# A bidirectional HGRN2 and Conformer encoder layer: the first step of a half head's preparation queued on VectorE behind the level-64 key update of the half head in work

## The chip, the cores and the metric

One core of one Trainium2 chip runs the whole layer as one program. The metric is the device time of one execution in microseconds (us). The kernel before was run three times: 1732.26, 1730.40 and 1727.42 us, a median of 1730.4 us.

## The reference, cut to what matters

The layer mixes 1024 positions of width 1024 in two parallel branches and then applies a gated feed-forward block. The part that this change concerns is the branch called HGRN2, a gated linear recurrence that is run over the sequence in both directions for each of 8 heads of width 128:

```python
def _chunk_gated_scan(q, k, v, lf):
    # S_t = diag(f_t) S_{t-1} + k_t v_t^T,  o_t = S_t^T q_t
    ...
    def step(state, inp):
        qb, kb, vb, lfb = inp
        a = jnp.cumsum(lfb, axis=2)
        diff = a[:, :, :, None, :] - a[:, :, None, :, :]
        decay = jnp.where(tril, jnp.exp(jnp.minimum(diff, 0.0)), 0.0)
        scores = jnp.einsum("bhtk,bhsk,bhtsk->bhts", qb, kb, decay)
        o = (jnp.einsum("bhts,bhsv->bhtv", scores, vb)
             + jnp.einsum("bhtk,bhkv->bhtv", qb * jnp.exp(a), state))
        ...
def _bi_hgrn2(q, v, z_fwd, z_bwd, lb_fwd, lb_bwd):
    ...
    o_fwd = _chunk_gated_scan(qh, heads(k_f), vh, heads(lf_f))
    o_bwd = flip(_chunk_gated_scan(flip(qh), flip(heads(k_b)), flip(vh), flip(heads(lf_b))))
    return o_fwd + o_bwd
```

The decay between two positions is the product of all forget gates between them. All else in the layer (projections, convolutions, feed-forward block, norms) is untouched by the change.

## The kernel before, in words

The kernel runs in stages: projections of the input with the convolution branch, then the scan of the 8 heads with the remaining dense projections between its pieces, then the merge, the output projection and the feed-forward block.

**The scan.** A head's 1024 positions are two halves of 512; the loop goes over 16 half heads, numbered 0 to 15 here. The chip's buffers carry the numbers of the program: the keys of half heads 3, 4, 5 and 6 are kG_787, kG_836, kG_896 and kG_949, their queries qF_823, qF_888, qF_936 and qF_1006. Each half head goes through a doubling scheme. At level h (1, 2, 4, ..., 64) pairs of neighbouring blocks of h positions meet: the keys are multiplied by the decay to the block's edge (`double_keys`, VectorE, line L1143 because all go through the helper `tt`), the queries likewise (`double_queries`), and the block totals `tb` are multiplied in pairs (`totals`). The updates of one half head's keys are a chain, each on the one before. In a row of the profile `kG<-kG,tb` is a key update, `qF<-qF,tb` a query update, `tb<-tb` or `tb<-f` totals.

**Who waits for it.** TensorE (PE) multiplies keys and queries of a level. For levels up to 16 it reads copies that ScalarE makes (`woven`, tiles A, L1175) before VectorE's next update; the products of the first four go into one PSUM bank `sc` (`level`, L1194), those of levels 8 and 16 into `ob`. Levels 32 and 64 are read from kG and qF themselves (`blocks`, L1280). After the level-64 key update, TensorE transposes the finished keys of both directions (`scan_states`, L1320, `tr<-ident,kG`), ScalarE copies the transposes, and TensorE forms the chunks' states from them (L1329).

**Three half heads at a time.** While half head i is in work (`scan_levels`, `scan_states`), half head i + 1 is in preparation (`scan_base`, held by the class `Base` as `ahead`) and half head i + 2 has its inputs loaded and makes its first step (`following`). The first step of `scan_base` ends at its first `yield`: it scales the two directions' keys (L1223), adds them (A<-kG), makes the level-1 queries and keys and the first totals (tb<-f). `between(n)` is called after each piece of half head i: it issues one or two pieces of dense projections (`dense.fill(FILL)`), one piece of the previous head's output, and one step of `ahead` for n below 4, of `following` at n = 4.

**What sets the order.** TensorE's order is the order in which the code is written (`manual_schedule`). For the other engines a scheduler orders the instructions of the program by its own costs, within what data and buffers allow; each engine then runs its instructions strictly in that order, and waits at the one in front. So the rows in which VectorE runs the steps of the three half heads are the scheduler's choice, unless an instruction is tied to another.

Of the kernel before, what the change touches and what calls it, by code (L numbers as in the profile page):

```python
# [37 lines left out]
def view(t, off, dims):  # L38

    return bass.AP(  # L40
        tensor=t.tensor,
        offset=t.offset + off,
        ap=[list(t.ap[0])] + [list(d) for d in dims],
    )
# [3 lines left out]
def tile_hybrid_encoder(  # L48
# [24 lines left out]
    V, A, G, T = nc.vector, nc.scalar, nc.gpsimd, nc.tensor  # L73
# [20 lines left out]
    def nm(s):  # L94
        uid[0] += 1
        return f"{s}_{uid[0]}"
# [3 lines left out]
    def bank(tag):  # L100
        return ps.tile([P, H], F32, tag=tag, name=nm(tag), bufs=BANKS[tag])

    def page(pool, tag, bufs, dt=F32):
        return pool.tile([P, H], dt, tag=tag, name=nm(tag), bufs=bufs)
# [64 lines left out]
    class Weights:  # L169
# [3 lines left out]
        def __init__(self, steps):  # L173
            self.parts = {}
            self.steps, self.wait = steps(self.parts), 0
            self.tick()
# [963 lines left out]
    G.memset(none, 0.0)  # L1140

    def tt(o, a, b, op=ALU.mult):
        V.tensor_tensor(o, a, b, op=op)  # L1143

    kscale = cp.tile([P, 2 * NH], F32, name="kscale")
    V.tensor_scalar(kscale, lbw[:, 3, :], DK**-0.5, None, op0=ALU.mult)
# [1 line left out]
    def c4(t):  # L1148
        return t.rearrange("p (c t) -> p c t", c=4)
# [18 lines left out]
    def pairs(t, h, other=H):  # L1168

        return view(t, 0, [[other + h, 2], [2 * h, H // (2 * h)], [1, h]])  # L1170

    def woven(t, h):

        t_h = page(hp, "A", 8)
        A.copy(pairs(t_h, h, 0), pairs(t, h))  # L1175
        return t_h

    def slot(b, n):
        return b[:, n * P : (n + 1) * P]

    def near(t):
        return t.rearrange("p (c t) -> p c t", c=4)

    def over(m):
        return view(m, 0, [[0, 4], [1, 32]])

    def each():
        for c in range(4):
            for g in range(0, P, 32):
                yield c * P + g, slice(g, g + 32), slice(32 * c, 32 * c + 32)  # L1190

    def level(b, A_t, Q_t):
        for at, g, o in each():
            T.matmul(b[g, o], A_t[:, at : at + 32], Q_t(at), start=True, stop=True)  # L1194

    def row(t):
        return lambda at: t[:, at : at + 32]

    def double_keys(kG, tb, h):
        n, nb = H // (2 * h), H // h  # L1200
        tt(pairs(kG, h), pairs(kG, h), view(tb, 1, [[nb - 1, 2], [2, n], [0, h]]))

    def double_queries(qF, q, tb, h):
        n, nb = H // (2 * h), H // h
        tt(pairs(qF, h), q, view(tb, nb + 1, [[-(nb + 1), 2], [2, n], [0, h]]))

    def totals(tb, h, to=None):
        n, nb = H // (2 * h), H // h
        tn = None
        if to is None:  # L1210
            tn = hp.tile([P, 2, n], F32, tag=f"tb{h}", name=nm("tb"), bufs=1 if h < 8 else 2)
            to = view(tn, 0, [[n, 2], [1, n]])
        tt(to, view(tb, 0, [[nb, 2], [2, n]]), view(tb, 1, [[nb, 2], [2, n]]))
        return tn

    def scan_base(ins):


        q, f, kG, ks = ins
        qF = hp.tile([P, 2, H], F32, tag="qF", name=nm("qF"), bufs=4)  # L1220
        D_t = hp.tile([P, 4, 32], F32, tag="D", name=nm("D"), bufs=3)
        for d in range(2):
            V.tensor_scalar(kG[:, d, :], kG[:, d, :], ks[:, d : d + 1], None, op0=ALU.mult)  # L1223
        k_d, Q1 = page(hp, "A", 8), page(hp, "A", 8)
        tt(k_d, kG[:, 0, :], kG[:, 1, :], ALU.add)
        A1 = woven(kG, 1)
        odd = H // 2
        tt(
            pairs(Q1, 1, 0),
            view(q, 0, [[1, 2], [2, odd], [1, 1]]),  # L1230
            view(f, H, [[1 - H, 2], [2, odd], [1, 1]]),
        )
        tt(
            view(qF, 1, [[H - 1, 2], [2, odd]]),
            view(q, 1, [[-1, 2], [2, odd]]),
            view(f, H + 1, [[-(H + 1), 2], [2, odd]]),
        )
        double_keys(kG, f, 1)
        double_queries(qF, pairs(Q1, 1, 0), f, 1)
        tb = totals(f, 1)  # L1240
        yield
        A2, Q2 = woven(kG, 2), woven(qF, 2)
        double_keys(kG, tb, 2)
        double_queries(qF, pairs(qF, 2), tb, 2)
        tb = totals(tb, 2)
        A4, Q4 = woven(kG, 4), woven(qF, 4)
        yield
        b = bank("sc")
        for n, (k_t, q_t) in enumerate(((k_d, q), (A1, Q1), (A2, Q2), (A4, Q4))):
            level(slot(b, n), k_t, row(q_t))  # L1250
        double_keys(kG, tb, 4)
        double_queries(qF, pairs(qF, 4), tb, 4)
        tb = totals(tb, 4)
        A8, Q8 = woven(kG, 8), woven(qF, 8)
        yield
        A.copy(D_t, near(slot(b, 3)))
        for n, m in enumerate((m_d, m_1, m_2)):
            V.copy_predicated(D_t, over(m), near(slot(b, n)))
        double_keys(kG, tb, 8)
        double_queries(qF, pairs(qF, 8), tb, 8)  # L1260
        tb = totals(tb, 8)
        A16, Q16 = woven(kG, 16), woven(qF, 16)
        yield
        double_keys(kG, tb, 16)
        double_queries(qF, pairs(qF, 16), tb, 16)
        tb = totals(tb, 16)
        yield qF, kG, tb, D_t, A8, Q8, A16, Q16

    def scan_levels(base, S_t, Tt):


        qF, kG, tb, D_t, A8, Q8, A16, Q16 = base

        def blocks(b, h):

            for c in range(0, H, P):
                for s0 in range(0, P, h):
                    t0 = s0 ^ h
                    d = s0 // h % 2
                    T.matmul(  # L1280
                        b[s0 : s0 + h, c + t0 : c + t0 + h],
                        kG[:, d, c + s0 : c + s0 + h],
                        qF[:, 1 - d, c + t0 : c + t0 + h],
                        start=True,
                        stop=True,
                    )

        def double(tb, h, to=None):
            double_keys(kG, tb, h)
            double_queries(qF, pairs(qF, h), tb, h)  # L1290
            return totals(tb, h, to)

        b = bank("ob")
        level(slot(b, 0), A8, row(Q8))
        level(slot(b, 1), A16, row(Q16))
        S_b = bank("sc")
        for at, g, _ in each():
            T.matmul(S_b[g, at : at + 32], none, none, start=True, stop=True)
        blocks(S_b, 32)
        for n, m in enumerate((m_8, m_16)):  # L1300
            V.copy_predicated(D_t, over(m), near(slot(b, n)))
        tb = double(tb, 32)
        yield
        yield
        b = S_b
        blocks(b, 64)
        double(tb, 64, view(Tt, 0, [[4, 2], [1, 4]]))
        A.copy(S_t, c4(b))
        for g in range(0, P, 32):
            G.dma_start(S_t[g : g + 32, :, g : g + 32], D_t[g : g + 32])  # L1310
        yield
# [92 lines left out]

    class Base:
        def __init__(self, ins):
            self.gen, self.val = scan_base(ins), None

        def step(self, n):
            while n > 0 and self.val is None:  # L1410
                self.val = next(self.gen)
                n -= 1

        def result(self):
# [33 lines left out]
    for h in range(NH):  # L1448
        Tt = hp.tile([P, 2, 2, 4], F32, tag="Tt", name=nm("Tt"), bufs=4)
        Sf = [hp.tile([P, 4, DK], F32, tag="st", name=nm("Sf"), bufs=4) for _ in range(2)]  # L1450
        Sb = [hp.tile([P, 4, DK], F32, tag="st", name=nm("Sb"), bufs=4) for _ in range(2)]
        kept = []
        for half in range(2):
# [13 lines left out]
            for n, _ in enumerate(scan_levels(base, S_t, Tt[:, half])):  # L1467
                if n == 1:
                    b = bank("tr")
# [5 lines left out]
            qF, kG = base[:2]  # L1475
# [514 lines left out]
    n = starts[-1] - per_seven - 12  # L1990
# [50 lines left out]
```

## Time and profile before

| quantity | value |
|---|---|
| the profiled execution's own time | 1733.97 us |
| its span, first to last instruction | 1732.2 us |
| ScalarE busy in the span | 826.1 us (48%) |
| GpSimd busy in the span | 206.5 us (12%) |
| mean granted TensorE clock | 0.996 |
| bytes read from and written to HBM | 201.40 and 87.03 MB |

The profiled execution is a run of its own beside the three timed ones; 1.8 us of its time lie outside the span. TensorE's rows need care: matmuls overlap in the pipeline and their ends are modelled, so an interval of idle TensorE is what is left after a modelled end. On VectorE one instruction starts some 0.08 us before the profile's end of the one before it, so what an instruction costs its queue is the distance of two starts, not the duration shown. The window from 495 to 865 us holds the scan.

### The profile page before, as it was taken

How to read it: one execution, taken by the hardware profiler on the slowest of the kernel's cores; microseconds unless marked ns; L12 is line 12 of the kernel's file. 1: busy time of each engine (PE TensorE's matmuls, PEld its weight loads, DVE VectorE, ACT ScalarE, POOL GpSimd, SP SyncE). 2: the span in 40 equal slices, each digit the busy share in tenths (PEclk: the TensorE clock that was granted, in tenths of full speed). 3: DMA queues.
4: the chain of work that ended last, by engine and by line, in shares of the span. 5: the costliest groups of instructions: out<-in, count | busy, mean ns of one | idle time of the engine just before them, and what ended most of it. 6: DMA issues, size and time to landing. Idle time of an engine off the chain costs nothing. (4 is left out here: it accounts for less than half of the span.)

```text
span 1732.2 us, 30782 instructions
## 1 busy us (share of the span) xinstructions
PE 1704.5 (98%) x11902; PEld 1416.5 (82%) x11902; DVE 1255.2 (72%) x1937; ACT 826.1 (48%) x1544; POOL 206.5 (12%) x249
## 2 busy tenths in 40 slices
PE   8999999999999999999999999999999999999998
PEld 6878888788788888888878888888888788888787
DVE  4599999746778888888566466666767776657864
ACT  7444443334566777776442245444334443542334
POOL 2211111100001111111100002011111111000110
PEclk9999999999999999999999999999999999999999
DMA  8778888854673434436579466567777777783842
GB/s 287 236 173 183 192 194 192 199 165 151 207 238 101 134 126 132 127 114 211 185 258 318 143 206 196 146 149 160 158 168 168 161 179 162 226 263 105 215 93 98
DMA packets 336585, 308.29 MB, mean 178 GB/s; under 512 B 17070, under 2 KB 248630, under 8 KB 336438
## 3 DMA queue, kind: packets, MB, share of 16 engines
q1 hardware_dynamic: 289590, 267.51, 48.9%
q0 software_dynamic: 46848, 38.81, 15.3%
q8 instruction: 93, 1.52, 0.4%
q14 instruction: 54, 0.44, 0.1%
HBM read 201.40 MB, written 87.03 MB: 167 GB/s over the span
## 5 line engine op out<-in xcount | busy, mean ns | idle before, releaser
L148 PE MATMUL mm<-hx,wp 128*128 128x512 f32 x1068 | 429.0, 402 | 5.9 <-ACT tm L850 2.5
L150 PE MATMUL mm<-hx,wp 128*128 128x512 f32 x1068 | 418.4, 392 | 1.0 <-DVE wp L124 0.9
L149 PE MATMUL mm<-hx,wp 128*128 128x512 f32 x1068 | 417.8, 391 | 0.5 <-DVE hx L124 0.5
L124 ACT CAST wp<-wr 128x1024 fp32r<-128x1024 f32 (+2 forms) x147 | 147.4, 1004 | 270.6 <-DMA wr<-wr 115.3
L148 PEld LDWEIGHTS mm<-hx,wp 128*128 128x128 f32 x1068 | 201.3, 188 | 50.8 <-ACT su L439 3.2
L150 PEld LDWEIGHTS mm<-hx,wp 128*128 128x128 f32 x1068 | 201.2, 188 | 47.2 <-DVE wp L124 4.4
L149 PEld LDWEIGHTS mm<-hx,wp 128*128 128x128 f32 x1068 | 201.6, 189 | 40.7 <-DVE hx L124 1.4
L124 DVE TENSOR_TENSOR wp<-wr,wp 128x1024 fp32r<-128x1024 f32 (+2 forms) x145 | 169.5, 1170 | 82.0 <-ACT wp L124 79.1
L1038 DVE SCALAR_TENSOR_TENSOR acc<-gl,v_b,acc 128x1024 f32<-128x1024 f32 x120 | 149.0, 1278 | 0.4
L439 ACT COPY su<-mm 128x512 f32<-128x512 f32 x82 | 47.7, 581 | 58.8 <-PE mm L150 58.7
L148 PE MATMUL tr<-hx,wp 128*128 128x512 f32 x180 | 70.5, 392 | 0.0
L150 PE MATMUL tr<-hx,wp 128*128 128x512 f32 x180 | 70.0, 389 | 0.0
L149 PE MATMUL tr<-hx,wp 128*128 128x512 f32 x180 | 70.0, 389 | 0.0
L1310 POOL DMA_DIRECT2D S<-D x64 | 35.5, 560 | 286.7 <-ACT jk L1375 127.7
L1143 DVE TENSOR_TENSOR qF<-qF,tb 128x512 f32<-128x512 f32 x96 | 65.5, 686 | 4.6 <-ACT A L1175 4.6
L1637 DVE SCALAR_TENSOR_TENSOR tm<-gp,v_a,tm 128x512 f32<-128x512 f32 x88 | 66.0, 750 | 3.8 <-ACT tm L1635 2.0
L124 ACT CAST wq<-sw 128x1024 fp32r<-128x1024 f32 x41 | 43.2, 1054 | 52.3 <-PE mm L149 43.0
L1143 DVE TENSOR_TENSOR kG<-kG,tb 128x512 f32<-128x512 f32 x96 | 65.2, 686 | 0.3
L148 PE MATMUL mm<-hy,wp 128*128 128x512 f32 x164 | 64.2, 391 | 0.0
L148 PE MATMUL sc<-hy,wq 128*128 128x512 f32 x164 | 64.2, 391 | 0.0
L150 PE MATMUL sc<-hy,wq 128*128 128x512 f32 x164 | 63.8, 389 | 0.0
L149 PE MATMUL mm<-hy,wp 128*128 128x512 f32 x164 | 63.8, 389 | 0.0
(373 smaller groups left out, 3679.4 us busy)
## 6 DMA issues: line engine op xcount, KB each, us to landing
wr<-in_w_in_dram SPq DMA_DIRECT2D x48, 512.0 KB, 4.3
wr<-in_ffn_w_up_dram SPq DMA_DIRECT2D x22, 512.0 KB, 6.2
sw<-in_w_in_dram SPq DMA_DIRECT2D x38, 256.0 KB
d_g<-ft SPq DMA_DIRECT2D x38, 256.0 KB, 3.4
sw<-in_ffn_w_up_dram SPq DMA_DIRECT2D x38, 256.0 KB, 4.1
sw<-in_ffn_w_up_dram POOLq DMA_DIRECT2D x19, 512.0 KB, 7.9
wr<-sw POOLq DMA_DIRECT2D x32, 256.0 KB, 3.8
wr<-wr POOLq DMA_DIRECT2D x32, 256.0 KB, 4.3
```

Source lines behind the costliest of these rows:

```text
L124: parts = A.copy(hi, src), eng.tensor_tensor(lo, src, hi.bitcast(F32), op=ALU.subtract)
L148: T.matmul(acc, whi[:, k, :], ahi, start=first, stop=False, skip_group_check=again)
L149: T.matmul(acc, whi[:, k, :], alo, start=False, stop=False, skip_group_check=again)
L150: T.matmul(acc, wlo[:, k, :], ahi, start=False, stop=last, skip_group_check=again)
L439: A.copy(t, acc)
L1038: V.scalar_tensor_tensor(acc, g[:, k : k + S], tap(k), acc, op0=ALU.mult, op1=ALU.add)
L1143: V.tensor_tensor(o, a, b, op=op)
L1310: G.dma_start(S_t[g : g + 32, :, g : g + 32], D_t[g : g + 32])
L1637: V.scalar_tensor_tensor(c, g[:, o + k : o + k + H], vec("fdw", k * NF + j), c, op0=ALU.mult, op1=ALU.add,)
```

## The change

The level-64 key update of the half head in work is remembered in a list of one entry. When a `Base` makes its first step, all instructions of that step that go to VectorE are tied behind it in VectorE's order. The tie is one of order alone: no semaphore is waited for, and no instruction is added or taken away.

```diff
     def tt(o, a, b, op=ALU.mult):
-        V.tensor_tensor(o, a, b, op=op)
+        return V.tensor_tensor(o, a, b, op=op)
+
+    last_keys = []
...
     def double_keys(kG, tb, h):
         n, nb = H // (2 * h), H // h
-        tt(pairs(kG, h), pairs(kG, h), view(tb, 1, [[nb - 1, 2], [2, n], [0, h]]))
+        return tt(pairs(kG, h), pairs(kG, h), view(tb, 1, [[nb - 1, 2], [2, n], [0, h]]))
...
-        def double(tb, h, to=None):
-            double_keys(kG, tb, h)
+        def double(tb, h, to=None, kept=None):
+            done = double_keys(kG, tb, h)
+            if kept is not None:
+                kept[:] = [done]
             double_queries(qF, pairs(qF, h), tb, h)
             return totals(tb, h, to)
...
-        double(tb, 64, view(Tt, 0, [[4, 2], [1, 4]]))
+        double(tb, 64, view(Tt, 0, [[4, 2], [1, 4]]), last_keys)
...
     class Base:
         def __init__(self, ins):
-            self.gen, self.val = scan_base(ins), None
+            self.gen, self.val, self.first = scan_base(ins), None, True

         def step(self, n):
             while n > 0 and self.val is None:
-                self.val = next(self.gen)
+                if self.first and last_keys:
+                    with tc.issue_after(last_keys[0].ins):
+                        self.val = next(self.gen)
+                else:
+                    self.val = next(self.gen)
+                self.first = False
                 n -= 1
```

The scheduler then orders VectorE and ScalarE anew throughout the scan; TensorE's and GpSimd's orders stay, and on the DMA queue of SP a few neighbouring loads and stores change places. Three places of VectorE's order show it.

**First place: the rows that end at half head 3's level-64 key update** (kG_787<-kG_787,tb_903), near 589 us of the trace. Half head 4 (kG_836, qF_888) is in preparation; f_895, q_894, tb_941, tb_964, qF_936, kG_896 and A_938 belong to half head 5's first step. Before:

```order
L1143 TENSOR_TENSOR kG_836_5324<-kG_836_5324,tb_911_5832 128x2x64x4
L124 TENSOR_TENSOR wp_907_5812<-wr_905_5809,wp_906_5811 128x1024
L1143 TENSOR_TENSOR qF_888_5695<-qF_888_5695,tb_911_5832 128x2x64x4
L1143 TENSOR_TENSOR kG_836_5324<-kG_836_5324,tb_919_5932 128x2x32x8
L1143 TENSOR_TENSOR qF_936_6041<-q_894_5710,f_895_5711 128x2x256
L1143 TENSOR_TENSOR tb_941_6054<-f_895_5711 128x512
L1143 TENSOR_TENSOR tb_964_6185<-tb_941_6054 128x256
L1398 SCALAR_TENSOR_TENSOR ev_917_5862<-tr_916_5857,v_a_1084,og_864_5495 128x512
L1143 TENSOR_TENSOR qF_888_5695<-qF_888_5695,tb_919_5932 128x2x32x8
L1143 TENSOR_TENSOR kG_836_5324<-kG_836_5324,tb_924_5974 128x2x16x16
L1143 TENSOR_TENSOR A_938_6045<-kG_896_5712 128x512
L1143 TENSOR_TENSOR kG_787_4993<-kG_787_4993,tb_903_5798 128x2x4x64
```

With the change:

```order
L1143 TENSOR_TENSOR kG_836_5324<-kG_836_5324,tb_893_5708 128x2x128x2
L1143 TENSOR_TENSOR qF_888_5695<-qF_888_5695,tb_893_5708 128x2x128x2
L124 TENSOR_TENSOR wp_907_5812<-wr_905_5809,wp_906_5811 128x1024
L1143 TENSOR_TENSOR kG_836_5324<-kG_836_5324,tb_911_5832 128x2x64x4
L1143 TENSOR_TENSOR qF_888_5695<-qF_888_5695,tb_911_5832 128x2x64x4
L1143 TENSOR_TENSOR kG_836_5324<-kG_836_5324,tb_919_5932 128x2x32x8
L1402 SCALAR_TENSOR_TENSOR ev_917_5862<-tr_916_5857,v_a_1084,og_864_5495 128x512
L1143 TENSOR_TENSOR qF_888_5695<-qF_888_5695,tb_919_5932 128x2x32x8
L1143 TENSOR_TENSOR kG_836_5324<-kG_836_5324,tb_924_5974 128x2x16x16
L1143 TENSOR_TENSOR qF_888_5695<-qF_888_5695,tb_924_5974 128x2x16x16
L1143 TENSOR_TENSOR kG_787_4993<-kG_787_4993,tb_903_5798 128x2x4x64
```

Four instructions of half head 5 (qF_936, tb_941, tb_964, A_938) are gone from ahead of the update. Two of half head 4 have come in: its level-2 key update (kG_836<-kG_836,tb_893), which before stood further up, ahead of half head 3's level-32 update, and its level-16 query update (qF_888<-qF_888,tb_924), which before stood behind.

**Second place: half head 5's first step itself**, on VectorE. Before, its first scaling stood directly behind half head 4's last totals (Tt_942):

```order
L1143 TENSOR_TENSOR kG_836_5324<-kG_836_5324,tb_893_5708 128x2x128x2
L1143 TENSOR_TENSOR tb_933_6012<-tb_924_5974 128x32
L1143 TENSOR_TENSOR tb_956_6149<-tb_933_6012 128x16
L1143 TENSOR_TENSOR Tt_942_6056<-tb_956_6149 128x8
L1223 TENSOR_SCALAR kG_896_5712<-kG_896_5712,kscale_4332 128x512
L1335 COPY Sf_830_5318<-sc_886_5664 128x128
```

With the change it stands behind the level-64 key update of half head 3:

```order
L1143 TENSOR_TENSOR kG_787_4993<-kG_787_4993,tb_903_5798 128x2x4x64
L1143 TENSOR_TENSOR qF_823_5302<-qF_823_5302,tb_903_5798 128x2x4x64
L1260 COPY_PREDICATED D_889_5696<-m_d_1507,sc_918_5865 128x128
L1402 SCALAR_TENSOR_TENSOR ev_923_5965<-tr_922_5960,v_a_1084,og_875_5620 128x512
L1260 COPY_PREDICATED D_889_5696<-m_1_1508,sc_918_5865 128x128
L1225 TENSOR_SCALAR kG_896_5712<-kG_896_5712,kscale_4332 128x512
L1260 COPY_PREDICATED D_889_5696<-m_2_1509,sc_918_5865 128x128
L1225 TENSOR_SCALAR kG_896_5712<-kG_896_5712,kscale_4332 128x512
L1143 TENSOR_TENSOR qF_936_6041<-q_894_5710,f_895_5711 128x2x256
```

The whole step has moved some twenty rows down, past half head 3's last updates.

**Third place: half head 6's level 2** (kG_949 and qF_1006 with tb_1011), while half head 5 (kG_896, qF_936) is in work, near 627 us. The query update there is followed by ScalarE's copy of it, which TensorE's products at L1194 read. Before:

```order
L1143 TENSOR_TENSOR kG_896_5712<-kG_896_5712,tb_998_6401 128x2x8x32
L1301 COPY_PREDICATED D_937_6042<-m_16_1511,ob_1019_6477 128x128
L1143 TENSOR_TENSOR qF_936_6041<-qF_936_6041,tb_998_6401 128x2x8x32
L1143 TENSOR_TENSOR qF_1006_6444<-qF_1006_6444,tb_1011_6457 128x2x128x2
L1143 TENSOR_TENSOR kG_949_6063<-kG_949_6063,tb_1024_6571 128x2x64x4
```

With the change:

```order
L1143 TENSOR_TENSOR kG_896_5712<-kG_896_5712,tb_998_6401 128x2x8x32
L1305 COPY_PREDICATED D_937_6042<-m_16_1511,ob_1019_6477 128x128
L1143 TENSOR_TENSOR qF_936_6041<-qF_936_6041,tb_998_6401 128x2x8x32
L1143 TENSOR_TENSOR kG_949_6063<-kG_949_6063,tb_1011_6457 128x2x128x2
L1143 TENSOR_TENSOR qF_1006_6444<-qF_1006_6444,tb_1011_6457 128x2x128x2
L1143 TENSOR_TENSOR kG_949_6063<-kG_949_6063,tb_1024_6571 128x2x64x4
```

The level-2 key update of half head 6, which before was done in the half head's first burst, now stands directly ahead of the query update. Over the whole program, the level-2 key update of the half head in preparation falls from ahead of the level-32 update of the half head in work to behind it in 3 of 14 cases (half heads 4, 6 and 8).

## The prediction

> **What bounds the kernel now.** I read the page first, then the busy times by stretch, then TensorE's waits, then VectorE's timeline at the waits found.
>
> ```profile
> span 1732.2 us, 30782 instructions
> PE 1704.5 (98%) x11902; PEld 1416.5 (82%) x11902; DVE 1255.2 (72%) x1937; ACT 826.1 (48%) x1544; POOL 206.5 (12%) x249
> ```
>
> TensorE (PE) is busy in all but 28 us of the span. A change of VectorE's order can take away idle TensorE time or add some, and nothing else. So the next view is where the idle time lies in the scan (us from the start, length, then the busy time of PE, PEld, DVE, ACT, POOL, the granted clock, DMA share, GB/s):
>
> ```profile
> 495.00:865.00 370.00, 366.16 (x5882) 314.74 (x5882) 303.45 (x660) 258.45 (x586) 48.50 (x78) 1.00 0.45 143
> 580.00:600.00 20.00, 17.97 (x339) 15.13 (x337) 19.83 (x44) 15.30 (x30) 2.25 (x4) 1.00 0.50 163
> 620.00:640.00 20.00, 19.56 (x345) 16.41 (x344) 16.30 (x33) 17.42 (x36) 2.26 (x5) 1.00 0.45 146
> 720.00:740.00 20.00, 18.62 (x254) 15.95 (x254) 18.38 (x44) 12.58 (x23) 2.26 (x4) 1.00 0.49 151
> PE tr L1320 <- DVE kG L1143: 3.8, 3, 2.0
> 589.83 0.66 PE L1320 MATMUL tr<-ident,kG 128*128 128x128 f32 x4 [2.03 <-DVE kG L1143]
> 634.08 0.66 PE L1320 MATMUL tr<-ident,kG 128*128 128x128 f32 x4 [0.44 <-DVE kG L1143]
> 721.56 0.66 PE L1320 MATMUL tr<-ident,kG 128*128 128x128 f32 x4 [1.38 <-DVE kG L1143]
> ```
>
> In the 370 us of the scan TensorE idles 370.00 - 366.16 = 3.84 us. The waits name it all: three times the transposes of finished keys (L1320) wait for VectorE's key update, 2.03 + 0.44 + 1.38 = 3.85 us. In the other 13 half heads this wait does not show. VectorE is busy 303.45 of 370 us: it has room on average, and is late only at these three places. What the change can win in the scan is therefore at most some 3.9 us, or 0.22% of the time. A difference of under 0.3% (5.2 us of 1730.4) is about what a measurement of this kernel can't tell from no change; the three runs before alone lie 4.8 us apart.
>
> **The change part by part.** No instruction is added or removed; the eight VectorE instructions of a first step (and with them later totals) move behind the level-64 key update. What such an instruction costs the queue is the distance of two starts:
>
> ```profile
> 569.88 0.69 DVE L1143 TENSOR_TENSOR kG<-kG,tb 128x512 f32<-128x512 f32 x1
> 570.49 0.40 DVE L1143 TENSOR_TENSOR tb<-tb 128x32 f32<-128x32 f32 x2
> ...
> 584.96 0.69 DVE L1143 TENSOR_TENSOR qF<-q,f 128x512 f32<-128x512 f32 x1
> 585.56 0.69 DVE L1143 TENSOR_TENSOR tb<-f 128x512 f32<-128x512 f32 x1
> 586.28 0.42 DVE L1143 TENSOR_TENSOR tb<-tb 128x256 f32<-128x256 f32 x1
> 586.62 0.74 DVE L1398 SCALAR_TENSOR_TENSOR ev<-tr,v_a,og 128x512 f32<-128x512 f32 x1
> ...
> 588.48 0.69 DVE L1143 TENSOR_TENSOR A<-kG 128x512 f32<-128x512 f32 x1
> 589.09 0.68 DVE L1143 TENSOR_TENSOR kG<-kG,tb 128x512 f32<-128x512 f32 x1
> ...
> 590.49 0.69 DVE L1143 TENSOR_TENSOR qF<-qF,tb 128x512 f32<-128x512 f32 x1
> 591.09 0.75 DVE L1398 SCALAR_TENSOR_TENSOR ev<-tr,v_a,og 128x512 f32<-128x512 f32 x1
> ```
>
> *First wait (half head 3).* The update that TensorE waits for starts at 589.09 and ends at 589.77; the transposes start at 589.83. Ahead of it four instructions leave: qF<-q,f 585.56 - 584.96 = 0.60, tb<-f 586.28 - 585.56 = 0.72, tb<-tb 586.62 - 586.28 = 0.34, A<-kG 589.09 - 588.48 = 0.61; together 2.27 us. Two come in, as the first place of the order shows: half head 4's level-2 key update (here at 569.88, 570.49 - 569.88 = 0.61) and its level-16 query update (here at 590.49, 591.09 - 590.49 = 0.60); together 1.21. Net 1.06 us earlier: the wait shrinks from 2.03 to 0.97. It does not go.
>
> *Second wait (half head 5).* The same three instructions of the following half head leave (0.60, 0.60 and 0.33 by the rows below), and one level-2 key update comes in (0.61): net 0.92 earlier, more than the 0.44 waited. Gain 0.44.
>
> ```profile
> 628.74 0.69 DVE L1143 TENSOR_TENSOR qF<-q,f 128x512 f32<-128x512 f32 x1
> 629.34 0.68 DVE L1143 TENSOR_TENSOR qF<-qF,tb 128x512 f32<-128x512 f32 x1
> 629.94 0.69 DVE L1143 TENSOR_TENSOR tb<-f 128x512 f32<-128x512 f32 x1
> 630.54 0.68 DVE L1143 TENSOR_TENSOR kG<-kG,tb 128x512 f32<-128x512 f32 x1
> ...
> 631.81 0.41 DVE L1143 TENSOR_TENSOR tb<-tb 128x256 f32<-128x256 f32 x1
> 632.14 0.68 DVE L1143 TENSOR_TENSOR qF<-qF,tb 128x512 f32<-128x512 f32 x1
> ```
>
> *Third wait (half head 9).* The same three leave and nothing comes in (the level-2 key update stood there already): some 1.5 us earlier against 1.38 waited. Gain 1.38. Sum of the gains: 1.06 + 0.44 + 1.38 = 2.88 us.
>
> *What is late next.* Each first step now starts later, and TensorE needs its fruits one half head on, in the products at L1194. The last of them reads ScalarE's copy of the level-2-updated queries. At two places this copy comes just in time already:
>
> ```profile
> 628.31 0.62 ACT L1175 COPY A<-qF 128x512 f32<-128x512 f32 x1 [1.17 <-PE tr L1396]
> 628.57 1.07 PE L1194 MATMUL sc<-A,A 128*32 128x32 f32 x96
> 760.09 0.60 ACT L1175 COPY A<-qF 128x512 f32<-128x512 f32 x1
> 760.33 1.05 PE L1194 MATMUL sc<-A,A 128*32 128x32 f32 x96
> ```
>
> The 96 products are three groups of some 0.29 us; the third starts near 628.57 + 0.58 = 629.15, and the copy ended at 628.31 + 0.62 = 628.93: 0.22 us of cover. At 760 it is 760.91 against 760.69, again 0.22. At the first of the two (half head 6, third place of the order) a level-2 key update of 0.61 us now stands directly ahead of the query update that is copied: the products wait 0.61 - 0.22 = some 0.4 us. At the second the order keeps that update where it was, but TensorE arrives earlier by what it has won; if VectorE and ScalarE do not move with it, it waits. The bounds of both: nothing, if the copies move up along with TensorE as their own waits for TensorE end sooner; at most the 2.88 us won, all handed back. I take the one count that the rows give, 0.4, for both: 0.8 us is given back.
>
> *ScalarE and DMA.* ScalarE's copies of the moved step follow it; ScalarE is busy 258.45 of 370 us and its other work (bank copies L802, weight casts L124) changes place with them by one or two rows, hidden by three PSUM banks of products in flight; without that cover one row late costs some 0.6 us, a copy's length. On SP's queue a few neighbouring loads and stores swap; the loads are for half heads not yet begun, so I cost them at nothing; a late one would cost at most one issue slot.
>
> Sum: 2.88 - 0.8 = 2.1 us saved. Against the profiled execution (1733.97 us, of it 1732.2 span) that is 1731.9; this execution lies 3.6 us over the median of the runs shown, so against the median it is 1730.4 - 2.1 = **1728.3 us**. The unknown cost leaves 0 to 3.9 us saved, 1726.5 to 1730.4, and two medians of three runs scatter by some 2 us more.
>
> **The rivals.**
>
> *Faster by more than 0.3%.* It needs more than the scan holds. Behind the scan TensorE stalls near 900 us and runs slowly after it:
>
> ```profile
> 899.00:901.00 2.00, 1.23 (x5) 0.51 (x3) 0.43 (x1) 1.08 (x2) 0.00 (x0) 1.00 0.95 315
> 901.00:907.00 6.00, 5.54 (x17) 4.05 (x17) 5.62 (x10) 1.63 (x3) 0.00 (x0) 0.72 1.09 357
> ```
>
> Idle 0.77 + 0.46 us, and at a granted clock of 0.72 a further 6 x 0.28 = 1.7: 2.9 us. Should all three waits go, nothing come back, and these loads and splits, released by a scan that VectorE finishes earlier, be ready in time, 3.85 + 2.9 = 6.8 us are saved: 1723.6. For it: VectorE's queue loses long stops (below). Against it: TensorE also arrives earlier, and the DMA engines are full there (share 0.95 and 1.09). [...]
>
> *Slower: the preparation is late in every half head.* The first step, some 4.6 us of VectorE (two scalings of 0.5 and six instructions of 0.6), starts later: half head 5's second scaling ran at 577.79 (row below) and would now stand behind 589.09. If the level-2 key update then falls in front of the copied query update everywhere, and no cover is left, each of 14 half heads loses 0.61: 8.5 - 2.88 = 5.7 us slower, 1736.1. The point from which it decides is the order: the update falls behind the level-32 update in 3 of 14. Against it speaks too that VectorE idles 370 - 303.45 = 66.5 us in the scan, 4 us per half head.
>
> *Slower by the same place: the queue stops at its head.*
>
> ```profile
> 577.79 0.49 DVE L1223 TENSOR_SCALAR kG<-kG,kscale 128x512 f32<-128x512 f32 x1 [3.51 <-ACT kG L1162]
> DVE kG L1223 <- ACT kG L1162: 25.3, 13, 4.6
> 585.10 0.69 PE L1280 MATMUL sc<-qF,kG 128*64 128x64 f32 x16
> ```
>
> VectorE stood 3.51 us for the scaling of a first step because ScalarE had not made its keys, with other work behind it; 25.3 us in 13 such waits. The level-64 update has a wait of its own: TensorE must have read the old keys (L1280). At half head 3 that ended at 585.79, the update starts at 589.09 and would start 1.06 us earlier: over 2 us of cover. If the cover were gone, the whole first step would stand behind it; I give it no time of its own, the rival above holds it. [...]
>
> *It does nothing for the time.* What is won at the three waits comes back in full at L1194 and at the next key updates: 1730.4.
>
> **How the numbers follow.** The forecast with its own range of 1726 to 1731: 0.55. All handed back: 0.10. Faster beyond 0.3% (under 1725.2): 0.23. Slower beyond 0.3% (over 1735.6): 0.12. So same is 0.65. The range 1722 to 1734 reaches into the faster rival as far as all three waits and the stall near 900 gone, and leaves the far ends of both rivals out, less than 2 in 10.
>
> **What would show it.** In the changed kernel's profile the waits of L1320 for kG should sum to about 1 us, most of it at half head 3 near 588 us; the two others should be gone. New waits of L1194 for copies A should show near 628 and 759 us, some 0.4 us each. TensorE's idle time in the scan should fall from 3.84 to about 2 us, VectorE's waits of L1223 for ScalarE well below 25.3 us, and the stages behind 865 us should be the same length. I am wrong if L1320 still waits 2 us at half head 3, if L1194 waits at most half heads, or if the time changes behind the scan.

## The result, and the profile after

The changed kernel took 1725.72 us (median of 22 runs, 1723.88 to 1734.86), the kernel before, in runs beside it, 1730.0 us (22 runs, 1726.81 to 1734.81). The ratio is 0.9979 with a 95% interval of 0.9971 to 0.9986: by it 3.6 us less, between 2.4 and 5.0 (the two medians lie 4.3 us apart). A second measurement of the same pair gave 0.9988 (0.9978 to 0.9997): 2.1 us less. Both are smaller than 0.3%, and both are clear of zero. A saving of 2.1 us and a time of 1728.3 us had been forecast; the median lies 2.6 us under that time, inside the wide range of 1722 to 1734 us and just below the narrower one of 1726 to 1731.

The page of the changed kernel's profile begins so:

```profile
span 1722.5 us, 30765 instructions
PE 1698.2 (99%) x11902; PEld 1414.3 (82%) x11902; DVE 1255.7 (73%) x1937; ACT 826.1 (48%) x1544; POOL 207.6 (12%) x249
```

The work is the same to the instruction (11902 matmuls, 1937 instructions of VectorE); only idle time has gone. The span is 9.7 us under that of the profile before, more than the medians differ, so the two profiled executions are not to be compared as a whole. The scan is: its window (columns as in the prediction: busy time of PE, PEld, DVE, ACT, POOL, clock, DMA share, GB/s), and TensorE's waits in it (engine, line, releaser: us in total, times, longest):

```profile
495.00:865.00 370.00, 368.08 (x5900) 316.67 (x5899) 301.18 (x657) 258.66 (x589) 49.68 (x78) 1.00 0.45 144
PE tr L1324 <- DVE kG L1143: 1.2, 2, 1.0
PE sc L1196 <- ACT A L1177: 0.8, 2, 0.5
```

TensorE idles 370.00 - 368.08 = 1.92 us where it idled 3.84. L1324 is what was L1320 before (the transposes of finished keys), L1196 what was L1194 (the products of copies A). TensorE's timeline at the places of the prediction:

```profile
586.94 0.66 PE L1324 MATMUL tr<-ident,kG 128*128 128x128 f32 x4 [1.01 <-DVE kG L1143]
...
626.86 0.46 PE L1196 MATMUL sc<-A,A 128*32 128x32 f32 x32 [0.28 <-ACT A L1177]
...
631.17 0.60 PE L1324 MATMUL tr<-ident,kG 128*128 128x128 f32 x4
...
717.25 0.66 PE L1324 MATMUL tr<-ident,kG 128*128 128x128 f32 x4
...
757.26 0.46 PE L1196 MATMUL sc<-A,A 128*32 128x32 f32 x32 [0.48 <-ACT A L1177]
...
761.90 0.66 PE L1324 MATMUL tr<-ident,kG 128*128 128x128 f32 x4 [0.16 <-DVE kG L1143]
```

At half head 3 the wait of 2.03 us is down to 1.01. At half heads 5 (631.17) and 9 (717.25) the rows have no wait any more, where there were 0.44 and 1.38. Two new waits for ScalarE's copies stand at 626.86 and 757.26, and one of 0.16 us at half head 11. VectorE's queue ahead of the first of these places reads, in its timeline:

```profile
580.44 1.22 DVE L124 TENSOR_TENSOR wp<-wr,wp 128x1024 fp32r<-128x1024 f32 x1
581.58 0.68 DVE L1143 TENSOR_TENSOR kG<-kG,tb 128x512 f32<-128x512 f32 x1
...
584.82 0.68 DVE L1143 TENSOR_TENSOR kG<-kG,tb 128x512 f32<-128x512 f32 x1
585.59 0.69 DVE L1143 TENSOR_TENSOR qF<-qF,tb 128x512 f32<-128x512 f32 x1
586.20 0.68 DVE L1143 TENSOR_TENSOR kG<-kG,tb 128x512 f32<-128x512 f32 x1
```

The last row is the level-64 key update of half head 3; the transposes start at its end. None of half head 5's first step stands ahead of it any more, and the level-16 query update of half head 4 does (585.59, 0.61 us to the next start). In this execution the whole scan lies 1.9 us earlier than in the one before (its first transposes, below), so of 589.09 - 586.20 = 2.89 us some 1.0 is the queue's own.

The queue does not run through without a stop. Ahead of these rows VectorE stands at the row f<-f for ScalarE, before and after:

```profile
579.60 0.69 DVE L1165 TENSOR_SCALAR f<-f 128x1024 f32<-128x1024 f32 x1 [0.77 <-ACT f L1164]
```

```profile
577.42 0.69 DVE L1167 TENSOR_SCALAR f<-f 128x1024 f32<-128x1024 f32 x1 [1.73 <-ACT f L1166]
```

From that row to the key update it is 589.09 - 579.60 = 9.49 us before and 586.20 - 577.42 = 8.78 us after, 0.71 us less. The other 0.3 us come from the stop: its end lies 8.20 us ahead of the moment when TensorE is ready for the transposes (589.83 - 2.03 = 587.80) before, and 8.51 us ahead of it (586.94 - 1.01 = 585.93) after.

VectorE's stops changed place rather than amount. Its waits over the whole run, after:

```profile
DVE qF L1143 <- ACT A L1177: 13.0, 10, 2.8
DVE f L1167 <- ACT f L1166: 11.2, 6, 3.6
DVE D L1305 <- PE ob L1196: 8.5, 5, 2.5
DVE kG L1225 <- ACT kG L1164: 4.0, 2, 3.5
```

The stop at the scalings fell from 25.3 to 4.0 us, and the other three rows have grown (the wait of qF for A was 4.6 us before, that of f 6.1, and the one of D had no row): VectorE stands for ScalarE, and at D for TensorE's bank `ob`, at a later instruction instead. Its busy time is 1255.7 us against 1255.2.

A length that does not depend on the window's edges is the distance from the first to the last transposes of keys. The grouped rows of that line (duration min/median/max in ns, then first and last start) before and after:

```profile
L1320 PE MATMUL mm<-ident,kG x64: 272/273/273, 526.9 to 852.1; 128*128 128x128 f32 x64
```

```profile
L1324 PE MATMUL mm<-ident,kG x64: 272/273/273, 525.0 to 848.7; 128*128 128x128 f32 x64
```

852.1 - 526.9 = 325.2 us before, 848.7 - 525.0 = 323.7 after: the scan is 1.5 us shorter by starts, 1.9 by idle time (whose ends are modelled). This distance serves below as the scan's length.

### The profile page after: what moved, and what is told of

Its sections match the earlier page's. It is cut to its first block, busy times and chain, and to the rows that moved or that the text cites. A ratio compares the mean times of both kernels' runs of the same rounds, so it can differ in the third digit from the quotient of the medians.

```text
span 1722.5 us, 30765 instructions
## 1 busy us (share of the span) xinstructions
PE 1698.2 (99%) x11902; PEld 1414.3 (82%) x11902; DVE 1255.7 (73%) x1937; ACT 826.1 (48%) x1544; POOL 207.6 (12%) x249
```

## The experiments

Two theories stood against each other. The **queue theory**, that of the prediction: TensorE waits for the level-64 key update by as much as rows of the next half head's first step stand ahead of it on VectorE; what counts is those rows at half heads 3, 5 and 9. The **rivals**: VectorE's stops at its queue's head (the 25.3 us at the scalings) are what costs; or the gain is spread over all half heads, or lies behind the scan.

All results in one table. Scan length is the last minus the first start in the row shown above, idle is 370 us less TensorE's busy time in 495 to 865. Time differences are ratios times 1730 us. Kernels of one group shared a chip and the runs of the kernel before.

| kernel | scan length | idle in the window | ratio (95% interval) | time against before |
|---|---|---|---|---|
| before | 325.2 | 3.84 | | |
| after | 323.7 | 1.92 | 0.9979 (0.9971 to 0.9986) | -3.6 |
| before_again, profile alone | 325.1 | 3.65 | | |
| after_again, profile alone | 323.7 | 1.94 | | |
| e1_scalings | 326.8 | 4.73 | 1.0000 (0.9991 to 1.001) | 0.0 |
| e2_rest | 323.7 | 1.85 | 0.9986 (0.9976 to 0.9995) | -2.4 |
| e3_three | 322.9 | 1.33 | 0.9975 (0.9963 to 0.9987) | -4.3 |
| e3_others | 325.7 | 4.02 | 0.9996 (0.9983 to 1.001) | -0.7 |
| e4_32 | 327.4 | 5.52 | 1.0011 (1.0001 to 1.0022) | +1.9 |
| f6_3579_last | 322.3 | 0.89 | 0.9976 (0.9965 to 0.9986) | -4.2 |
| before_control | 325.1 | 3.78 | 1.0003 (0.999 to 1.0015) | +0.5 |
| after_control | 323.7 | 1.98 | 0.9988 (0.9978 to 0.9997) | -2.1 |
| e3_three_again | 322.9 | 1.31 | 0.9982 (0.9971 to 0.9994) | -3.1 |
| f6_again | 322.3 | 1.15 | 0.9971 (0.9961 to 0.9981) | -5.0 |

### The two kernels once more

Both unchanged, a profile each, to see which of their differences repeat.

> The kernel before, profiled a second time. Queue theory (the change acts on the three waits of L1320 alone): the same three waits of L1320 for kG near 590, 634 and 722 us, 2.0, 0.4 and 1.4 us within 0.2, and TensorE idle 3.8 us in 495 to 865 us, as these waits hang on VectorE's order and not on chance; the stretches ahead of 495 us and behind 865 us may differ by 2 to 4 us from the first profile. Rival (the change also makes the stages behind the scan faster): the slow clock near 901 to 907 us (0.72 in the first profile) and the four waits of TensorE behind ScalarE's copies su between 1186 and 1380 us show again.

> The changed kernel, profiled a second time. Queue theory: TensorE idle 1.9 us within 0.2 in the scan, of it 1.0 at L1324 near 587 us and 0.8 at two waits of L1196. Rival (the stages behind the scan are faster by the change): no slow clock near 900 us and no waits behind copies su between 1180 and 1375 us again, so that the stretch behind the scan again takes some 5 us less than in the kernel before; if it is chance, some of these stalls come back.

The scan repeats: 325.1 and 323.7 us, 3.65 and 1.94 idle, with the same waits. What lies ahead of it and behind it does not: from the last transposes to the end of the span it was 1732.2 - 852.1 = 880.1 and 1722.5 - 848.7 = 873.8 in the first two profiles, and 876.3 and 876.1 in these two. The 6 us by which the first two differ there were mostly chance.

### Only the scalings tied, and all but the scalings

`e1_scalings` ties the two scalings of a first step behind the level-64 key update and leaves its other rows free; `e2_rest` does the opposite. `tied()` is the change's own tie.

```diff
# e1_scalings, in scan_base
-        for d in range(2):
-            V.tensor_scalar(kG[:, d, :], kG[:, d, :], ks[:, d : d + 1], None, op0=ALU.mult)
+        with tied():
+            for d in range(2):
+                V.tensor_scalar(kG[:, d, :], kG[:, d, :], ks[:, d : d + 1], None, op0=ALU.mult)
```

```diff
# e2_rest, in scan_base, behind the scalings
+        with tied():
             k_d, Q1 = page(hp, "A", 8), page(hp, "A", 8)
             tt(k_d, kG[:, 0, :], kG[:, 1, :], ALU.add)
             A1 = woven(kG, 1)
...
             double_keys(kG, f, 1)
             double_queries(qF, pairs(Q1, 1, 0), f, 1)
             tb = totals(f, 1)
```

> Only the two key scalings of a first step are tied behind the level-64 key update; its query products and totals stay free. Queue theory (what counts is how many instructions stand ahead of the level-64 key update): qF<-q,f, tb<-f and tb<-tb stand ahead of it again, 1.66 us at half head 3 and 1.54 at half heads 5 and 9, so the three waits of L1320 stay within 0.6 us of before or grow, new waits of L1194 come on top as in the change, and TensorE idles 4 to 6 us in the scan: 0 to 2 us slower than before. Rival (what counts is that VectorE no longer stops for ScalarE at the scalings, 25.3 us of stops before, 4.0 after): with the scalings moved the whole gain is there, TensorE idles some 2 us in the scan and the time is that of the change, 0.2% under before.

> All of a first step but the two key scalings is tied behind the level-64 key update. Queue theory: the same instructions leave the stretch ahead of the update as in the change (at half head 3 the level-2 key update stays where it was before, 0.6 us less in the stretch, the level-16 query update comes in), so the waits of L1320 fall to some 1 us at half head 3 and under 0.6 at the others, and with no level-2 update in front of the copy at half head 6 the wait of L1194 there is under 0.3 us: TensorE idles some 2 us in the scan, as in the change. Rival (the stops at the scalings): the stops stay near 25 us, and nothing is gained: 3.8 us idle, time as before.

The scan's window of `e1_scalings`, TensorE's two waits in it, and VectorE's wait at the scalings in the whole run (L1328 is the line of the transposes here, L1229 that of the scalings):

```profile
495.00:865.00 370.00, 365.27 (x5876) 313.68 (x5875) 299.76 (x657) 257.61 (x582) 49.06 (x78) 1.00 0.45 142
PE tr L1328 <- DVE kG L1143: 3.8, 4, 1.8
PE sc L1196 <- ACT A L1177: 0.8, 2, 0.5
DVE kG L1229 <- ACT kG L1164: 4.1, 3, 3.5
```

The same rows of `e2_rest`:

```profile
495.00:865.00 370.00, 368.15 (x5899) 316.46 (x5898) 300.83 (x657) 257.32 (x587) 49.12 (x78) 1.00 0.46 144
PE tr L1328 <- DVE kG L1143: 1.6, 3, 0.7
PE sc L1196 <- ACT A L1177: 0.2, 1, 0.2
DVE kG L1228 <- ACT kG L1164: 20.3, 8, 3.6
```

The first takes the stops at the scalings away (25.3 to 4.1 us; those at f grow from 6.1 to 15.6) and gains nothing: TensorE still waits 3.8 us for the keys, and the 0.8 us for copies A come on top. The second leaves 20.3 us of them and has the change's whole gain in the scan. The stops at the scalings are thus not what cost time, and the rival that rests on them falls. The rows that counted are the products and totals that stood between the scalings and the late update.

### Tied at three half heads, and at the eleven others

```diff
# e3_three, in Base.step; turn[0] is the half head in work
-                if self.first and last_keys:
+                if self.first and last_keys and turn[0] in (3, 5, 9):
```

```diff
# e3_others
-                if self.first and last_keys:
+                if self.first and last_keys and turn[0] in (0, 1, 2, 4, 6, 7, 8, 10, 11, 12, 13):
```

> The first step of the half head that follows is tied behind the level-64 key update only while half heads 3, 5 and 9 are in work; in the eleven other half heads it stays as before. Queue theory (the change gains only by the rows that leave from ahead of the three late level-64 updates): the idle time of TensorE in the scan window 495 to 865 us falls from 3.7-3.8 us of the kernel before to 1.6-2.4, as with the whole change (1.92); the transposes wait some 1 us near 589 and up to 0.7 us near 634 or 721; time 1.5 to 4 us under the kernel before, ratio 0.9975 to 0.999. VectorE's stops at the scalings stay near 20 us. Rival (the gain is spread over all half heads, or lies behind the scan and comes from VectorE finishing the scan earlier): three of fourteen moved steps give a fifth of the gain or none, under 1 us, ratio above 0.9993.

> The counterpart: the first step is tied in the eleven other half heads, and left as before while half heads 3, 5 and 9 are in work. Queue theory: the three late updates keep their rows, the transposes still wait some 2, 0.5 and 1.4 us near 589, 634 and 721, idle time in the scan 3.5 to 4.6 us, no gain: ratio 0.9995 to 1.0005. Rival (spread over all half heads, or behind the scan): most of the change's 3.6 us appears here, ratio 0.998 to 0.9985, although the idle time in the scan stays.

The scan's window and waits of `e3_three`:

```profile
495.00:865.00 370.00, 368.67 (x5902) 316.98 (x5901) 301.06 (x658) 258.46 (x592) 48.41 (x78) 1.00 0.46 144
PE tr L1325 <- DVE kG L1143: 1.3, 3, 0.5
```

and of `e3_others`:

```profile
495.00:865.00 370.00, 365.98 (x5888) 314.91 (x5887) 300.83 (x657) 257.28 (x584) 49.44 (x78) 1.00 0.46 143
PE tr L1325 <- DVE kG L1143: 3.3, 3, 1.8
PE sc L1197 <- ACT A L1178: 0.8, 2, 0.5
```

TensorE's transposes in `e3_three` at half heads 5 and 9:

```profile
630.73 0.66 PE L1325 MATMUL tr<-ident,kG 128*128 128x128 f32 x4 [0.36 <-DVE kG L1143]
717.29 0.66 PE L1325 MATMUL tr<-ident,kG 128*128 128x128 f32 x4 [0.44 <-DVE kG L1143]
```

and in `e3_others` at half head 5:

```profile
631.65 0.60 PE L1325 MATMUL tr<-ident,kG 128*128 128x128 f32 x4
```

Three ties of fourteen carry all of the scan's gain, and a little more than all: 1.33 us idle, less than the 1.6 expected at best. Eleven ties carry none (4.02 idle, ratio 0.9996). The waits show why. The two waits for copies A (0.8 us), which the change pays at 626.86 and 757.26, come with the eleven needless ties and are absent with the three. And the transposes of half head 3 wait 0.50 us here, not 1.01: half head 4's own first step is not tied, and in VectorE's order its level-2 key update (0.61 us) stands ahead of half head 3's level-32 update again, as it did before, instead of between that and the late one. A spread over all half heads falls with this pair. Half head 5 does not fit, though. Tied alone with 3 and 9 it still waits 0.36 us, and left untied in `e3_others`, where 0.5 us was expected, it does not wait at all: its wait hangs on more than its own tie (see below). Half head 9 keeps 0.44 us in `e3_three`, where the whole change left none.

### The tie one level sooner

```diff
# e4_32: what is remembered is the level-32 key update
-        tb = double(tb, 32)
+        tb = double(tb, 32, None, last_keys)
...
-        double(tb, 64, view(Tt, 0, [[4, 2], [1, 4]]), last_keys)
+        double(tb, 64, view(Tt, 0, [[4, 2], [1, 4]]))
```

> The tie is put one level sooner: the first step stands behind the level-32 key update of the half head in work, so it may again run ahead of the level-64 one, in every half head. The scalings are then also between the two updates. Queue theory: five to six instructions of the first step (two scalings of 0.5 us, qF<-q,f and tb<-f of 0.6 each) stand ahead of the level-64 update in more half heads than before; the transposes wait at four to seven half heads, 5 to 8 us idle in the scan, time 1 to 4 us over the kernel before, ratio 1.0005 to 1.0025. Rival (any tie that bundles the first step and takes away VectorE's stops at the scalings gains): stops at the scalings fall below 10 us and the time falls like the change's, ratio 0.998 to 0.999.

```profile
495.00:865.00 370.00, 364.48 (x5865) 312.58 (x5864) 303.97 (x661) 258.20 (x582) 48.38 (x78) 1.00 0.45 141
PE tr L1324 <- DVE kG L1143: 5.5, 5, 1.7
```

These rows (the window, TensorE's only wait in it) show five half heads waiting 5.5 us together, against three and 3.8 before. With the first step pushed into the gap right ahead of the level-64 update the same instructions cost time: 1.7 us more idle in the scan, 1.9 us by the ratio (0.2 to 3.8). The queue theory holds in the losing direction too; a tie as such does not help.

### A version with more rows taken away

```diff
# f6_3579_last, in Base; self.count is the number of the step
+        def tied(self):
+            if self.count == 0:
+                return turn[0] in (3, 5, 7, 9, 13)
+            return self.count == 4 and turn[0] in (3, 5, 9, 13)
```

> A version that the queue theory suggests: the first step is tied while half heads 3, 5, 7, 9 and 13 are in work, and while 3, 5, 9 and 13 are in work the last step (level 16) of the half head in preparation is tied behind the level-64 update as well, so that more rows leave from ahead of it. Queue theory: the wait of the transposes at half head 3 goes from 1 us to under 0.3; idle time in the scan 1.0 to 1.6 us, some of it a new wait for the level-16 products (bank ob) of half head 4; time 2.5 to 5 us under the kernel before, 0 to 1.5 under the change. Rival (what leaves from ahead of one update comes back as a wait for the preparation): idle time in the scan 2 us or more, time no better than the change's, new waits at bank ob or sc.

```profile
495.00:865.00 370.00, 369.11 (x5905) 317.61 (x5904) 300.29 (x660) 259.24 (x589) 48.41 (x78) 1.00 0.46 145
PE tr L1325 <- DVE kG L1143: 0.6, 2, 0.4
PE ob L1375 <- DVE Sb L1437: 0.3, 1, 0.3
```

Of the scan's 3.84 us, 0.89 is left, a little under the 1.0 expected at best. Nothing waits at half head 3, from ahead of which two level-16 updates of half head 4 have gone as well, as expected. The wait of 0.3 us in bank `ob` is not the expected one for the level-16 products: L1375 multiplies a head's outputs out of its states, and at 602.50 it waits for VectorE's update of the backward state Sb. Half heads 7 and 9 keep 0.15 and 0.45 us. It is the shortest scan of all the versions.

### Controls, and the better versions beside the change

> The kernel before, timed against itself, as a control of the interval. Both theories: ratio 1.000 within 0.001; the scan from the first to the last transposes of keys is 325.6 us long again, 3.7 us of idle TensorE in the window 495 to 865.

> The changed kernel, timed once more. What is open is whether the 1.7 us by which the first median gain (3.6 us) exceeds the scan's (1.9 us) belongs to the change. Theory that the change acts in the scan alone: gain 1 to 3 us, ratio 0.9983 to 0.9994, scan 1.5 us shorter from first to last transposes of keys, the rest of the program as scattered as before. Rival (the change also moves the stages behind the scan): ratio 0.9975 to 0.9982 again, and the part behind the last transposes shorter by 1.5 us or more in the profile.

> The version that is tied only while half heads 3, 5 and 9 are in work, beside the changed kernel on one chip. Queue theory: its scan idles 1.3 us against the change's 1.9, so its time lies 0.6 us under the change's, too little to be told: ratio 0.9976 to 0.9992. Rival (fewer ties, smaller gain): 1 us or more over the change.

> The version that ties at half heads 3, 5, 7, 9 and 13 and takes the level-16 step of the half head in preparation along at 3, 5, 9 and 13. Queue theory: its scan idles 0.9 us, 1 us under the change; its time 0.5 to 1.5 us under the change's, ratio 0.997 to 0.9988, so perhaps the fastest of the four but hardly to be told from the version with three ties. Rival (the gain comes back behind the scan): the time of the kernel before within 1 us, ratio above 0.9994.

The kernel before against itself gives 1.0003 within 0.0013, so the interval can be trusted at this size. The change gains 2.1 us this time, the three ties 3.1, the last version 5.0: in the order of their scan lengths, but with intervals that overlap (0.9978 to 0.9997, 0.9971 to 0.9994, 0.9961 to 0.9981). That the last is faster than the change is likely, not shown.

On what lies behind the scan the two signs that were set for the rival disagree: the ratio, 0.9988, went against it, but the part behind the last transposes was 1723.4 - 849.1 = 874.3 us after and 1729.8 - 850.1 = 879.7 in the control before.

## Why the prediction was right

**What bounds the kernel: right.** The three waits of the transposes are the scan's only idle time, they repeat from profile to profile within 0.2 us, and taking most of their cause away (`f6_3579_last`) leaves 0.89 us.

**First wait: right to 0.04 us, in part by luck.** Four rows out, two in, net 1.06 earlier and 0.97 left was the count; 1.01 is left. But the rows counted give 0.71 of the 1.02 us, as shown above: with the change two of the rows start 0.77 instead of some 0.60 us after the one in front (that at 585.59 is shown). The other 0.31 came from VectorE's stop at f, which ends earlier against TensorE and was not in the count. That the two rows that came in kept the wait from going is shown: with one of them back in its old place (`e3_three`) 0.50 is left, and with the level-16 step gone too (`f6_3579_last`) nothing.

**Second wait: gone, but not by the rows counted.** In `e3_others` half head 5 is not tied; from f to the key update VectorE takes 8.02 us there, as before (8.01), and yet nothing waits. In `e3_three` it is tied, and 0.36 us are left. What `e3_others` shares with the change is that the row f<-f stands 8.9 us ahead of TensorE's arrival at the transposes, where it stood 8.3 ahead before and in `e3_three`. Of these 0.6 us, 0.28 are TensorE's own new wait at 626.86, which makes it arrive later: that much of the gain only changed place.

**Third wait: gone, with nothing to spare.** Counted were 1.5 us earlier against 1.38 waited; the update comes 1.37 us earlier against TensorE's arrival (716.51 against 717.25 after, 720.82 against 720.18 before). VectorE now stops 0.31 us for a copy of ScalarE within these rows (713.31); in return half head 9's level-32 key update runs ahead of the stop at f (706.91 against 708.83). In `e3_three` the same three rows leave, but that update stands behind f, and 0.44 us are left. The count missed both.

**What is given back: right in place and sum, wrong in the cause.** 0.28 + 0.48 = 0.76 us at 626.86 and 757.26, against 0.4 + 0.4 near 628 and 759. The forecast gave the second to TensorE arriving earlier while the copies stay. `e3_three` contradicts that: TensorE arrives earlier there too, the copy moves up with it and starts 0.01 us ahead of the products (0.03 behind them before), and nothing waits; in `e3_others`, which wins almost nothing, the same 0.48 us show. What differs is ScalarE's order. Before, a bank copy (ev) stood ahead of the copy of the queries:

```profile
759.60 0.58 ACT L802 ACTIVATE ev<-mm 128x512 f32<-128x512 f32 x1
```

With the change it is a weight cast, which takes 0.95 us of the queue instead of 0.49, while TensorE's products start at 755.73:

```profile
755.65 1.04 ACT L124 CAST wp<-wr 128x1024 fp32r<-128x1024 f32 x1
756.60 0.61 ACT L1177 COPY A<-qF 128x512 f32<-128x512 f32 x1
```

And in `e3_three` it is the bank copy again:

```profile
755.29 0.59 ACT L802 ACTIVATE ev<-mm 128x512 f32<-128x512 f32 x1
755.77 0.61 ACT L1178 COPY A<-qF 128x512 f32<-128x512 f32 x1
755.78 0.46 PE L1197 MATMUL sc<-q,A 128*32 128x32 f32 x32
```

The cast accounts for 0.46 us of the copy's delay; some 0.4 more came from the key copy ahead of both, which waits for VectorE's update and starts 0.61 us ahead of the products where it stood 0.99 ahead. At the first place the level-2 key update does stand in front, as forecast, but ScalarE adds to it:

```profile
625.71 0.58 ACT L1482 COPY v<-tr 128x512 f32<-128x512 f32 x1
626.19 0.62 ACT L1177 COPY A<-qF 128x512 f32<-128x512 f32 x1
```

The queries are ready at 625.75, but ScalarE has begun the copy of v, which before stood behind (628.84). Without it the copy would have ended near 626.4, when the third group of products was due (625.79 + 0.58 = 626.37). By this estimate VectorE's later update only uses up the cover of 0.22 us, and the wait itself is ScalarE's row. So the term that failed is ScalarE's: its rows that change place were taken as hidden and costed at nothing, and they carry a good part of both waits (`e3_three` shows it at the second place, at the first it is an estimate). That the sum of 0.8 came out is luck. A wait of 0.16 us at half head 11 was not foreseen: TensorE arrives there earlier by what it has won, and the update does not.

**The sum: right for the scan, on the low side for the whole.** 2.1 us forecast, 1.9 by idle time and 1.5 by starts in the scan. The time gives 3.6 and 2.1. The agreement in the scan is closer than that of the parts, whose errors cancel.

**That nothing changes behind the scan: not borne out, and open.** The time of every tied version that was measured is below what its scan length alone would give: by 2.1 and 0.6 us for the change, 1.6 and 0.9 for the two parts, 2.0, 0.8 and 1.2 for the three and the eleven, 0.3 one level sooner, 1.3 and 2.1 for the last, a mean of 1.3 us (kernels of one group share the runs of before, so these are four measurements rather than ten). `e1_scalings` and `e3_others`, which gain nothing in the scan, show it as well. The part behind the last transposes was 880.1, 876.3 and 879.7 us in the three profiles of the kernel before, and 873.6 to 876.9 in the eleven of tied versions. TensorE idles 12.5 to 14.4 us of that part in the three and 10.6 to 13.4 in the eleven (means 13.4 and 11.7). So some 1 us is probably won outside the scan's length; the ranges overlap. It is not the stall near 900 us that the rival "faster" named. The stretch from 880 to 915 in the control of the kernel before:

```profile
880.00:915.00 35.00, 32.60 (x141) 25.49 (x140) 26.12 (x38) 13.91 (x21) 0.00 (x0) 1.00 0.92 294
```

and in the two profiles of the changed kernel, the first and the last:

```profile
880.00:915.00 35.00, 33.11 (x145) 26.72 (x144) 26.70 (x39) 13.01 (x20) 0.00 (x0) 1.00 0.93 298
```

```profile
880.00:915.00 35.00, 33.30 (x145) 26.31 (x144) 26.32 (x38) 13.20 (x20) 0.00 (x0) 1.00 0.94 294
```

Idle there were 1.93, 1.96 and 2.40 us in the three profiles of before and 1.89, 2.33 and 1.70 in the three of after: the stall is still there. Nor need it be an order of instructions: in `e3_three` every engine's order is that of the kernel before, row for row, from half head 12's preparation to the end. Where this microsecond comes from was not settled.

**The rivals.** Faster by over 0.3%: its first half came about in part (two of three waits gone), its second half, the stall, did not. Slower, the preparation late everywhere: the level-2 update fell in front at few places, as the order said, and all the waits for copies came to 0.76 us. The queue stopping at its head: the stops moved to other rows (13.0, 11.2 and 8.5 us), and those at the scalings had cost nothing, as `e1_scalings` and `e2_rest` show from both sides. The forecast's warning that a late first step could be held by the level-64 update did not come true: that update is not held up here (in the changed kernel's scan, 495 to 865 us, key updates wait 2.5 us for copies A, none for TensorE). All handed back: of the 2.84 us won at the three waits 0.92 was.

## What to carry to other kernels

When one engine waits for a certain instruction of another, count which rows stand ahead of that instruction in the other's queue, by distances of starts, back to that queue's last stop, and which rows come in when some leave. Then look at what the new order makes that queue itself wait for, and at the third engine between the two. Here the count named the right places and the sum, but in single places it was off by 0.3 to 0.4 us (half head 3's stretch 0.71 for 1.06; `e3_three`, 0.36 and 0.44 left where it gives none), while 25 us of stops at the scalings on the same queue were worth nothing. Tie only where the wait is: three ties left a shorter scan than fourteen (322.9 against 323.7 us; the times do not tell them apart), because the needless eleven make other work late. And compare a stage by its own first and last instruction, which repeated to 0.1 us here, since the rest of the program varies by more than the whole effect.

## What the runs showed of the hardware

The scan's length repeats to 0.1 us in all profiles of one kernel (325.2, 325.1, 325.1 before; 323.7 three times after). Ahead of the scan the same program varies by 3 us (its first transposes at 525.0, 526.9 and 528.2 in the kernel before), and behind it by 4.

The slow clock behind the scan, 0.72 from 901 to 907 us in the first profile of before, which the prediction priced at 1.7 us, did not come again: over 900 to 910 us the granted clock was 0.83 in that profile and 1.00 in the thirteen others. The 0.72 is a mean: by single microseconds the granted clock there is 1.00 up to 903 and then 0.55, 0.50, 0.50 and 0.74, so half for some 3.4 us (estimate from these four). Ahead of it TensorE idles 0.77, 0.22 and 0.23 us. Over 880 to 915 the control of the same kernel idles 2.40 us against the first one's 1.93, its longest piece 1.11 us, at a granted clock of 1.00 (row above); in `after` and `after_again` pieces of 1.20 and 1.66 us stand there, at 1.00 as well. Around the 2.03 us wait in the scan of the first profile, from 580 to 600 us, it was 1.00 too. So idle pieces of 1.11 to 2.03 us stood in these profiles at an unchanged clock, and the dip came behind pieces of 0.77 us and less; what set it off was not shown.
